# Eight-core transformer layer: small inputs in one transfer, earlier weight halves, layer norms by pieces, the D term from channel-major x

## The chip, the cores and the metric

The kernel runs on all 8 cores of one Trainium2 chip. Each core works on its own share of the batch, and the shares do not communicate. The metric is the device time of the slowest core, in microseconds (us), from its first to its last instruction. Each core has five engines: TensorE (PE in the profile, its weight loads PEld), VectorE (DVE), ScalarE (ACT), GpSimd (POOL) and SyncE (SP, which here only issues transfers).

Some executions fall into a slow state, in which one die shows a lower granted clock and the time is some per cent longer.

## The reference, cut to what matters

One layer with two groups of tokens that share all weights. Per core there are 1024 latent tokens and 512 context tokens (two sequences of 256). In the kernel, group `GB` is the latent one (row tiles 0 to 7, chunks 0 and 1 of x) and `GA` the context one (row tiles 8 to 11, chunk 2).

```python
h    = x * (1 + sc1) + sh1                    # shift, scale, gate: silu(cond) @ w_ada + b_ada
q, k, v, g, z, xbc, dt = split(h @ w_in)
o_ret = silu(g) * rms_norm(bidir_scan(q, k, v))            # 4 retention heads, chunkwise scan
xs, B, C = split(silu(depthwise_conv(xbc)))
y     = bidir_scan(C, B, xs * dt) + d_skip * xs            # 8 SSD heads; d_skip * xs is the "D term"
o_ssd = rms_norm(y * silu(z)) * ssd_norm_w
x     = layer_norm(ALPHA * x + g1 * (concat(o_ret, o_ssd) @ w_out), ln1_g, ln1_b)      # LN1
h2    = x * (1 + sc2) + sh2
x     = layer_norm(ALPHA * x + g2 * ((silu(h2 @ w_gate) * (h2 @ w_up)) @ w_down), ln2_g, ln2_b)   # LN2
```

## The kernel before

The kernel is a Python program that first collects operations with their reads and writes, then orders them by a list scheduler of its own, and lays all tiles into one arena of SBUF. The tables `LV` (priorities, lower first), `RING` (how many buffers a tile rotates through) and `LD` (which event starts a load) tune the result. I call order plus addresses *the plan*. It is fixed when the kernel is built, so it can be read by building the kernel, without a chip. Where I say "the built kernel" below, that is what was read.

Two tiles whose lifetimes do not overlap in the plan may share addresses, and the later one then waits for every operation on the earlier one:

```python
old, new = (b, c) if t1 <= u0 else (c, b)        # two tiles that share addresses
for f in firsts[new]:
    extra.setdefault(f.idx, set()).update(old.ops)
```

The start, cut: transfers on SyncE's queue in program order, and those that GpSimd issues when their `after` is done.

```python
P.dma(SP, cols, ...); P.dma(SP, cst, ...)         # [cut] constants from DRAM
ada_f32(2)                                        # w_ada slab 2, two halves
xT_load(2, 0); half_load("w_in0", w0, w_in_d[0], 0)
P.dma(SP, smalls, ...); P.dma(SP, w_dtf, ...)     # small inputs
xT_load(0, 0); ada_f32(3); xT_load(2, 1)
o_w0 = half_load("w_in0", w0, w_in_d[0], 1); xT_load(0, 1)
w_in[1] = slab_load("w_in1", ..., after=[o_w0])
ada[0] = slab_load("ada0", ..., after=[xTo[(0, 1)]])
ada[1] = slab_load("ada1", ..., after=[w_in[1][1]])
xT_load(1, 0, after=[ada[0][1]]); xT_load(1, 1, after=[ada[0][1]])   # the last x chunk
```

The residual and the normalisation, the same code for LN1 (groups of four tiles) and LN2:

```python
def residual(dst, banks, xres, gate, s, i):
    for half in range(2):
        hs = slice(half * 512, half * 512 + 512)
        tt(dst[:, hs], banks[half], gate[:, hs], ALU.mult)
        stt(dst[:, hs], xres[:, hs], ALPHA, dst[:, hs], ALU.mult, ALU.add, accum_out=s[:, half, i:i + 1])
    act(rjn(), dst, AF.Square, accum_out=s[:, 2, i:i + 1])         # rjn(): output that nobody reads
def normalise(dsts, s):                                            # one chain of small steps for four tiles
    # [cut] six small VectorE steps on 128x4
    tt(c[7], c[6], mhalf[:, 0:1].to_broadcast([128, n]), ALU.pow, POOL)
    stt(c[8], c[3], -1.0, c[7], ALU.mult, ALU.mult)
    # [cut] affine(dst) by halves
```

After the context tiles' LN1 come 32 transposes, and then the feed-forward's first matmuls for the context. These are the *filler*: plenty of TensorE work that needs nothing from the latent group, to be run while the latent group's retention waits on other engines.

## Time and profile before

Median 744.0 us (743.6 to 745.7). The view of cores:

```profile
core 3: 744.4 us, clock 0.964
core 7: 729.0 us, clock 0.979
```

The windows view of core 3, the slowest. Columns: the stretch and its length, then busy us (and instruction count) of PE, PEld, DVE, ACT, POOL, then the granted TensorE clock, DMA share and GB/s.

```profile
0.00:40.00 40.00, 13.21 (x108) 6.35 (x109) 22.16 (x93) 19.21 (x32) 2.67 (x12) 0.90 0.90 275
40.00:60.00 20.00, 20.00 (x166) 9.97 (x165) 8.34 (x25) 10.47 (x22) 1.58 (x3) 0.94 1.01 157
60.00:80.00 20.00, 6.38 (x113) 3.94 (x111) 5.73 (x18) 6.19 (x10) 2.54 (x11) 0.74 0.95 207
80.00:150.00 70.00, 69.14 (x504) 39.20 (x505) 45.32 (x109) 56.18 (x92) 30.17 (x65) 0.98 0.56 108
150.00:300.00 150.00, 135.07 (x1175) 78.77 (x1172) 120.18 (x198) 82.33 (x129) 84.20 (x97) 0.94 0.54 104
300.00:340.00 40.00, 35.21 (x289) 21.61 (x288) 36.99 (x69) 26.83 (x39) 23.95 (x22) 1.00 0.80 177
340.00:400.00 60.00, 57.82 (x330) 31.56 (x329) 44.62 (x98) 32.83 (x50) 15.26 (x17) 1.00 0.27 72
```

Read it as a list of where TensorE stands idle: 26.8 us in the first 40, 13.6 between 60 and 80 (the *hole*, with DMA at 0.95), 14.9 between 150 and 300, 4.8 between 300 and 340. From 408 us on it is dense.

The chain of waits says why the hole is there. Columns: start, length, what was waited for or done.

```profile
10.56 28.18 DMA arena<-xT
39.34 15.80 DMA arena<-w_ada
55.79 22.66 DMA arena<-xT
80.12 37.16 PE psum L634 x258
```

The last x chunk is under way until 78.5 us, and TensorE starts dense work on it at 80.

The end, from the timeline (start, length, engine, line, operation, output<-input, count, and in brackets the idle time before it and what ended it):

```profile
725.78 3.62 PE L634 MATMUL psum<-arena 128*128 128x512 bf16 x16
736.93 0.55 POOL L684 TENSOR_TENSOR arena<-arena 128x1 f32<-128x1 f32 x1 [0.43 <-DVE arena L684]
737.95 0.81 ACT L659 ACTIVATE arena<-arena 128x512 f32<-128x512 f32 x1 [3.75 <-DVE arena L698]
738.90 3.36 POOL L684 TENSOR_TENSOR arena<-arena 128x512 f32<-128x512 f32 x2 [1.43 <-ACT arena L659]
```

The last matmul ends at 729.4 us and the span at 744.4: a bare tail of 15.0 us.

### The profile page before, as it was taken

What the parts mean: (1) busy time and instruction counts of PE and PEld (TensorE: products, weight loads), DVE (VectorE), ACT (ScalarE), POOL (GpSimd) and SP (SyncE); (2) the same over time, 40 slices, a digit from 0 to 9 for tenths busy, and PEclk for the clock granted to TensorE, in tenths of its full rate; (3) what the DMA queues carried; (4) which work ended last, traced back from release to release, by engine and by line L of the source; (5) the groups of instructions that cost most, each with busy time, mean ns of one, the idle gap of its engine ahead of it and who ended that gap; (6) DMA issues with size and microseconds to landing.
All of it is one profiled execution on the core that took longest, in us unless ns stands there. A gap on an engine that the chain in (4) does not pass through costs nothing.

```text
span 744.4 us, 13000 instructions; the slowest of 8 cores (729.0 to 744.4 us)
## 1 busy us (share of the span) xinstructions
PE 666.2 (89%) x4212; PEld 342.3 (46%) x4212; DVE 404.5 (54%) x817; ACT 302.2 (41%) x478; POOL 291.4 (39%) x312
## 2 busy tenths in 40 slices
PE   0595699999978988989999999999999999999991
PEld 0243455545643456546445444444444444444440
DVE  6533249879876887898587212121121211366865
ACT  2654698686673333587447211111111110132121
POOL 0001315696364355566101299800000000059876
PEclk9888799999998998999999999999999999999996
DMA  8999726681697063980035133545300046002212
GB/s 241 333 145 220 147 37 113 143 169 26 120 156 131 2 126 75 251 173 30 29 113 114 57 58 57 113 82 106 82 1 1 1 106 163 1 28 85 86 58 85
DMA packets 15043, 75.68 MB, mean 102 GB/s; under 512 B 2960, under 2 KB 3216, under 8 KB 8320
## 3 DMA queue, kind: packets, MB, share of 16 engines
q0 software_dynamic: 5440, 40.77, 31.1%
q1 hardware_dynamic: 9536, 34.07, 14.0%
q8 instruction: 36, 0.59, 0.3%
q14 instruction: 31, 0.25, 0.1%
HBM read 107.03 MB, written 8.40 MB: 155 GB/s over the span
## 4 chain that ended last, share of the span: by engine, by line
PE 64%; DMA 12%; issue 8%; DVE 7%; POOL 4%; ACT 1%; SPq 1%; DVEq 0%; POOLq 0%; ACTq 0%
PE psum L634 64%; DMA arena<-xT 7%; DVE arena L684 4%; POOL arena L684 4%; DMA arena<-w_ada 4%; DVE arena L698 1%; SPq L191 1%; ACT arena L659 1%; DMA arena<-arena 1%; PE psum L637 1%; DVE arena L719 1%; DVE arena L722 1%; DVE arena L709 0%; DVEq L518 0%; POOL arena L191 0%
## 5 line engine op out<-in xcount | busy, mean ns | idle before, releaser
L634 PE MATMUL psum<-arena 128*128 128x512 bf16 (+6 forms) x4104 | 655.2, 318 | 63.0 <-ACT arena L659 29.5
L634 PEld LDWEIGHTS psum<-arena 128*128 128x128 bf16 (+1 forms) x4104 | 330.8, 99 | 384.0 <-issue 100.5
L684 POOL TENSOR_TENSOR arena<-arena 128x512 f32<-128x512 f32 (+6 forms) x204 | 257.4, 1282 | 185.1 <-DVE arena L684 116.3
L659 ACT ACTIVATE arena<-psum 128x512 bf16<-128x512 f32 (+2 forms) x180 | 99.8, 571 | 222.5 <-PE psum L634 204.3
L684 DVE TENSOR_TENSOR arena<-arena,psum 128x512 bf16<-128x512 bf16 (+3 forms) x134 | 86.6, 653 | 181.0 <-PE psum L634 175.8
L659 ACT ACTIVATE arena<-arena 128x512 bf16<-128x512 f32 (+8 forms) x156 | 107.5, 717 | 174.4 <-DVE arena L698 117.8
L684 DVE TENSOR_TENSOR arena<-psum,arena 128x512 bf16<-128x512 f32 (+5 forms) x202 | 127.8, 650 | 57.4 <-PE psum L634 48.1
L659 ACT ACT_TABLE_LOAD x48 | 61.6, 1283 | 26.2 <-PE psum L634 20.7
L698 DVE SCALAR_TENSOR_TENSOR arena<-arena 128x512 f32<-128x512 f32 (+2 forms) x60 | 43.9, 732 | 15.2 <-POOL arena L684 11.6
L684 DVE TENSOR_TENSOR arena<-arena 128x1 f32<-128x1 f32 (+10 forms) x87 | 38.6, 444 | 10.2 <-PE psum L634 3.2
L191 POOL DMA_DIRECT2D arena<-w_down x4 | 2.2, 538 | 101.5 <-PE psum L634 101.5
L659 ACT ACTIVATE arena<-psum,arena 128x512 bf16<-128x512 f32 (+2 forms) x58 | 35.9, 650 | 13.4 <-PE psum L634 8.8
L191 POOL DMA_DIRECT2D arena<-w_in x10 | 5.9, 590 | 57.5 <-DMA arena<-w_in 34.4
L709 DVE CAST arena<-psum 128x512 bf16<-128x512 f32 (+2 forms) x29 | 17.7, 622 | 17.7 <-PE psum L634 15.4
L709 DVE CAST arena<-arena 128x512 bf16<-128x512 f32 (+8 forms) x39 | 21.5, 557 | 10.7 <-DMA arena<-w_ada 4.3
L191 POOL DMA_DIRECT2D arena<-w_gu x11 | 6.4, 578 | 39.3 <-issue 20.7
L709 POOL CAST arena<-arena 128x2 bf16<-128x2 f32 x48 | 8.5, 220 | 33.8 <-DVE arena L709 16.4
L719 DVE SCALAR_TENSOR_TENSOR arena<-arena 128x512 f32<-128x512 f32 x25 | 19.6, 828 | 0.7
L690 DVE TENSOR_SCALAR arena<-arena 128x128 bf16<-128x128 f32 (+6 forms) x79 | 16.6, 260 | 5.0 <-ACT arena L659 4.1
L722 DVE TENSOR_SCALAR arena<-arena 128x512 bf16<-128x512 f32 x27 | 12.8, 510 | 11.6 <-DMA arena<-xT 11.5
L1279 DVE COPY_PREDICATED psum<-arena,psum 128x512 f32<-128x512 uint16 x24 | 16.6, 691 | 3.0 <-PE psum L634 2.7
L637 PE MATMUL psum<-arena 128*128 128x128 f32 (+1 forms) x108 | 14.4, 275 | 0.2 <-DVE arena L684 0.2
(20 smaller groups left out, 58.1 us busy)
## 6 DMA issues: line engine op xcount, KB each, us to landing
arena<-w_gu POOLq DMA_DIRECT2D x11, 1024.0 KB, 10.5
arena<-w_in POOLq DMA_DIRECT2D x10, 1024.0 KB, 11.8
arena<-w_ada POOLq DMA_DIRECT2D x10, 1024.0 KB, 15.2
arena<-xT SPq DMA_DIRECT2D x6, 1024.0 KB, 20.0
arena<-x SPq DMA_DIRECT2D x12, 512.0 KB, 4.9
arena<-w_down POOLq DMA_DIRECT2D x4, 1408.0 KB, 15.9
y<-arena SPq DMA_DIRECT2D x11, 512.0 KB, 2.7
arena<-w_ada SPq DMA_DIRECT2D x4, 1024.0 KB, 15.3
```

The source lines that it names most:

```text
L191: o = self.add({eng: (0.9 if eng == POOL else 0.45, lambda e: e.dma_start(out=R(out), in_=R(in_)))}, [in_], [out], after=after)
L634: return P.add({PE: (c, lambda e: e.matmul(R(out), lhsT=R(lhsT), rhs=R(rhs), start=start, stop=stop))}, [lhsT, rhs], [out])
L637: return P.add({PE: (0.12, lambda e: e.transpose(out=R(out), in_=R(in_), identity=R(ident_f)))}, [in_, ident_f], [out])
L659: fn = lambda e: e.activation(out=R(out), in_=R(in_), func=func, **{k: R(v) for k, v in kw.items()})
L684: fn = lambda e: e.tensor_tensor(out=R(out), in0=R(in0), in1=R(in1), op=op)
L690: fn = lambda e: e.tensor_scalar(out=R(out), in0=R(in0), scalar1=R(s1), scalar2=None, op0=op0)
L698: fn = lambda e: e.scalar_tensor_tensor(out=R(out), in0=R(in0), scalar=R(scalar), in1=R(in1), op0=op0, op1=op1, **{k: R(v) for k, v in kw. ...
L709: alts[g] = (vcost(g, out, [in_], "copy"), lambda e: e.tensor_copy(out=R(out), in_=R(in_)))
L719: lambda e: e.scalar_tensor_tensor(out=R(out), in0=R(in_), scalar=R(scale), in1=R(bias).to_broadcast([128, n_]), op0=ALU.mult, op1=ALU.add))
L722: lambda e: e.tensor_scalar(out=R(out), in0=R(in_), scalar1=R(scale), scalar2=R(bias), op0=ALU.mult, op1=ALU.add))
L1279: P.add({DVE: (0.7, lambda e, eb=eb, ef=ef, mk_=mk_: e.copy_predicated(R(eb), R(mk_), R(ef)))}, [mk_, ef, eb], [eb])
```

## The change

Intent: take small transfers and constants out of the queue at the start; load all weights that the first two chunks need before the last x chunk, so that the hole is filled; make the last tile's LN2 short; halve the matmuls of the D term. The new tiles did not fit beside the old plan, so rings, priorities and triggers were tuned again. The core of the diff, with cuts marked:

```diff
@@ start
-    P.dma(SP, cst, cf_d[:, 0:392])
+    iota(diff, 1, 0, -1, 0.5); ...; ts(ident_f, diff, 0.0, ALU.is_equal)      # [cut] constants made on chip
+    half_load("ada2", b, w_ada_d[2], 0)
+    P.dma(SP, cols, cols_d[:, :])                                  # all small inputs in one
+    ada[2] = (b, half_load("ada2", b, w_ada_d[2], 1))
-    w_in[1] = slab_load("w_in1", w_in_d[1], 4096, after=[o_w0])
-    ada[0] = slab_load("ada0", w_ada_d[0], 4096, after=[xTo[(0, 1)]])
-    ada[1] = slab_load("ada1", w_ada_d[1], 4096, after=[w_in[1][1]])
-    xT_load(1, 0, after=[ada[0][1]])
+    w_in[1] = slab_load("w_in1", w_in_d[1], 4096, after=[xTo[(2, 1)]])
+    ada[0] = slab_load("ada0", w_ada_d[0], 4096, after=[xTo[(2, 1)]])
+    ada[1] = slab_load("ada1", w_ada_d[1], 4096, after=[xTo[(2, 1)]])
+    for q in range(2):                                             # chunk 1, behind them on POOL's queue
+        xTo[(1, q)] = P.dma(POOL, xT[(1, q)], ..., after=[xTo[(2, 1)]])
@@ first projections: both slabs of chunks 2 and 0 before chunk 1
+    for ck in (2, 0): EV["p0" + "BxA"[ck]] = proj(0, ck)
+    for ck in (2, 0): EV["p1" + "BxA"[ck]] = proj(1, ck)
+    proj(0, 1); EV["p1C"] = proj(1, 1)
@@ D term
-        mm(y[:, h * 64:h * 64 + 64], dI3[:, h, :], xs_tm[t][:, h * 64:h * 64 + 64], False, True)    # 8 per tile
+        mm(y[:, c * 128:c * 128 + 128], xsT[(g, c)][:, tok], dI[:, c * 128:c * 128 + 128], True, False)   # 4 per tile
@@ LN1: by tile
+            s, junk = rst(), rjn()
+            for half in range(2):
+                piece(x1[t], banks[half], xr, gate, H[half], s, half, junk)    # square of half a row
+            moments(s, 2)                                                      # small steps on 128x1
+            tt(col(s, S_RSTD), col(s, S_MSQ), mhalf[:, 0:1], ALU.pow, POOL)
+            # [cut] affine by halves
@@ LN2: last tile in pieces of 512, 256, 256 columns
+            act(col(s, S_LN), col(s, S_NVAR), AF.Ln, scale=-1.0)
+            act(col(s, S_RSTD), col(s, S_LN), AF.Exp, scale=-0.5)
+            stt(w[:, hs], u[t][:, hs], col(s, S_MEAN), ln2[:, hs], ALU.subtract, ALU.mult)
+            stt(u[t][:, hs], w[:, hs], col(s, S_RSTD), ln2[...], ALU.mult, ALU.add)
@@ tables (cut)
-RING = dict(... yb=1, xw=3, Sd=3, ... hB=3, ... kt=2, ... xr=3)
+RING = dict(... yb=3, xw=2, Sd=2, ... hB=2, ... kt=3, ... xr=2)
-LD = dict(... xr1="b1", xr0="oA", ...)      # x rows for the context residual: latent head 1's projections done
+LD = dict(... xr1="b2", xr0="b3", ...)      # now: latent head 2's
-OPT = dict(rope="")
+OPT = dict(rope="q")
```

## The prediction

> **What bounds it now.** The view of cores: 729.0 to 744.4 us; core 3 is slowest. Its page has TensorE busy 666 of 744 us, so 78 us idle. Windows and timeline of core 3 place them:
> - Start: dense work proper begins at 36.9 us; TensorE is busy 13.2 of the first 40 us, DMA share near 1: transfer-bound.
> - Hole, 60 to 80 us: busy 6.4 of 20, DMA share 0.95. TensorE waits for a scaled x chunk; the last xT transfer, queued beside the second w_ada slab, lands at 78.5 us. Core 7, the quickest, is busy 12.9 there.
> - 150 to 400 us: about 22 us idle in pieces, VectorE 80 to 90% busy.
> - 408 to 729 us: dense, 0.2155 us per 512-column matmul. Nothing to win.
> - Tail: the last matmul ends at 729.4, the span at 744.4: 15 us. Residual pieces, a 1.06 us square, small VectorE steps, a POOL power, a 0.8 us affine, two multiply/add pairs (1.7 us per POOL step), the store.
>
> **The change, costed.**
> 1. Start: 196 KB of constants, the row and w_dt transfers leave the queue; cols goes behind the first w_ada half. At the 322 GB/s of 10 to 20 us, everything comes about 1 us earlier. The 786 KB selector load goes too, but nothing waited for it after 79 us.
> 2. Hole: both shift slabs of w_ada and w_in's second slab come before the last x chunk; the second slab's projection of chunk 0 (32 x 0.2155 = 6.9 us) and the context convolutions (80 x about 0.11 = 8.6 us) can run before it. The dense run from 37 should reach about 78 us, when chunk 1 lands. Gain about 12 us on the slowest core, 7 on a quick one, including a cold start: the Trainium skill, "TensorE: Matmul & The Clock Gate", Part 1, says that an idle array falls to half clock and needs about 3.4 us to warm; the trace agrees (matmuls 0.43 us apart after 22 and 37 us). Against it: POOL-issued loads start beside the last SP-issued halves and may cost 1 to 2 us at 37.
> 3. D term: 96 64-column matmuls become 48 128-column ones: about 1 us of TensorE.
> 4. LN1 by tile; new priorities, rings, load triggers; rope's q halves on ScalarE and POOL: 0 to 5 us, could be negative. I take 2.
> 5. Tail: 256-column residual 0.9, square 0.65, small steps 0.5, Ln and Exp 0.6 (no table load between them at 22 us), VectorE pieces 3, store 2: about 8 us against 15. Gain 6 to 7, fully exposed. POOL's multiplies leave, so VectorE's 1.1 to 1.8 us steps should take 0.7: the Trainium skill, "SBUF — State Buffer", "Who interferes with whom", says VectorE with two SBUF inputs contends with a POOL operation that reads SBUF.
>
> Sum: 1 + 12 + 1 + 2 + 6.5, about 22. 744 - 22 = **722 us**, 8 in 10 within 709 to 735. Faster by over 2% (below 729): 0.75; within 2%: 0.22; slower: 0.03.
>
> **Right or wrong in the profile.** Windows 60 to 80: TensorE over 17 of 20 busy on the slowest core, cores closer together. First dense run still from 36 to 38 us. Tail 7 to 9 us from last matmul to end. TensorE busy about 663 us. Last stretch: no 512-wide POOL operations. Idle of 150 to 400: 15 to 24 us.
>
> **What would make it wrong.** The filled hole is given back in the mixed stage because VectorE, not TensorE, bounds it there; new waits on weights whose triggers moved; w_in's second half slowed by sharing; denser TensorE work lowering the granted clock; a table load in the tail.

## More of the kernel before

The experiments' texts call the latent group "batch".

One more stretch, for comparison with after: TensorE between the end of the head projections and the context's transposes (the group with f32 128x128 tiles).

```profile
336.09 2.83 PE L634 MATMUL psum<-arena 128*128 128x128 bf16 x46 [2.00 <-DVE arena L684]
338.76 0.61 PE L637 MATMUL psum<-arena 128*128 128x128 f32 x4
```

TensorE waits 2.0 us here, the longest wait in the 20 us before the transposes, which start at 338.8 us.

## The result, and the profile after

After: 734.5 us median (734.1 to 738.0). The ratio to before is 0.988 (0.985 to 0.991). Ratios here are the mean time of one kernel's fast runs over that of the other's fast runs of the same rounds, so not quite the ratio of the medians quoted. The gain is 9.5 us, where 22 were forecast: the time is inside the range, at its upper edge, but "within 2%".

```profile
core 1: 733.4 us, clock 0.969
```

The windows of core 1, the slowest of after, with the same columns as before:

```profile
0.00:40.00 40.00, 14.66 (x109) 6.74 (x110) 25.87 (x88) 16.74 (x30) 10.61 (x23) 0.91 0.93 282
40.00:60.00 20.00, 20.00 (x172) 10.33 (x171) 11.73 (x32) 12.16 (x21) 1.52 (x3) 1.00 1.00 209
60.00:80.00 20.00, 16.68 (x189) 11.32 (x188) 8.72 (x27) 14.16 (x24) 8.30 (x45) 0.83 1.02 197
80.00:150.00 70.00, 69.71 (x508) 38.91 (x506) 47.20 (x112) 63.75 (x100) 31.28 (x38) 1.00 0.40 84
150.00:300.00 150.00, 136.46 (x1197) 82.73 (x1197) 119.58 (x203) 83.82 (x131) 92.61 (x104) 0.99 0.73 128
300.00:340.00 40.00, 21.97 (x167) 13.38 (x165) 30.68 (x71) 18.87 (x37) 18.96 (x18) 0.74 0.27 89
340.00:400.00 60.00, 59.15 (x309) 32.11 (x309) 47.04 (x126) 35.84 (x65) 12.64 (x15) 0.97 0.33 89
```

Subtract the PE column of before from it, stretch by stretch. To 150 us TensorE has done 12.3 us more: the hole is filled (16.7 of 20, where 6.4 were). Between 150 and 300 it gains 1.4. **Between 300 and 340 it loses 13.2.** To 400 it regains 1.3. The TensorE work in all is 1.6 us less (the D term; 666.2 and 664.6 on the two pages), and the tail is 7.6 us shorter. The sum, 12.3 + 1.4 - 13.2 + 1.3 + 1.6 + 7.6 = 11.0, is the difference of the two spans (744.4 - 733.4). The loss at 300 to 340 us is not that of one core: TensorE is busy 34.4 to 35.3 of these 40 us on the eight cores of before, and 20.7 to 22.0 on the eight of after.

The start and the hole in the chain of waits of after:

```profile
7.20 28.11 DMA arena<-w_in
...
36.59 27.07 PE psum L632 x252
```

Dense work starts at 36.6 us, 0.3 before that of before (36.9), and no wait for the last x chunk is left in this stretch.

The tail of after, from the timeline:

```profile
721.76 4.20 PE L632 MATMUL psum<-arena 128*128 128x256 bf16 x37
728.25 2.99 DVE L696 SCALAR_TENSOR_TENSOR arena<-arena 128x512 f32<-128x512 f32 x6
728.43 0.50 ACT L657 ACTIVATE arena<-arena 128x1 f32<-128x1 f32 x2 [0.79 <-DVE arena L690]
```

The last matmul ends at 725.96; 7.4 us follow. Ln and Exp take 0.50 us together, with no table load between them. The Trainium skill, "ScalarE: Activation LUTs", section "Table sets: the hidden batching unit", says that one set holds both; the trace agrees.

And the new hole, from the timeline of 300 to 350 us. DVE L696 are the residuals, ACT 128x512 bf16<-128x512 f32 with arena on both sides the context tiles' squares:

```profile
306.23 1.75 DVE L696 SCALAR_TENSOR_TENSOR arena<-arena 128x512 f32<-128x512 f32 x1
...
312.69 0.68 DVE L696 SCALAR_TENSOR_TENSOR arena<-arena 128x512 f32<-128x512 f32 x1
...
327.76 0.63 ACT L657 ACTIVATE arena<-arena 128x512 bf16<-128x512 f32 x1 [1.33 <-issue]
...
336.99 0.58 ACT L657 ACTIVATE arena<-psum 128x512 bf16<-128x512 f32 x1
...
337.81 2.29 PE L632 MATMUL psum<-arena 128*128 128x512 bf16 x13 [11.09 <-DVE arena L690]
...
340.70 5.64 PE L635 MATMUL psum<-arena 128*128 128x128 f32 x32 [0.59 <-DVE arena L717]
```

TensorE idles 11.1 us before 337.8. The profile puts the wait down to VectorE, but the operation that ended just before is the ScalarE read of PSUM at 336.99 (retention's own). It stood in ScalarE's queue behind squares and affines of the context's LN1. The built kernel confirms both: the first of these 13 matmuls reads what that ScalarE operation writes, and ScalarE's order has the eight squares and three affines of the context's LN1 before it. The first square starts at 327.8 us although its residual was ready at 308.0 (306.23 + 1.75). The context's transposes start at 340.7, 1.9 us *later* than before (338.8), although TensorE came 12 us earlier to this point. So the filler is not there when the head projections run out.

### The profile page after: what moved, and what is told of

Same layout as the page of the kernel before. It is cut to its first block, busy times and chain, and to the rows that moved or that the text cites. A ratio compares the mean times of both kernels' runs of the same rounds, so it can differ in the third digit from the quotient of the medians.

```text
span 733.4 us, 13130 instructions; the slowest of 8 cores (722.6 to 733.4 us)
## 1 busy us (share of the span) xinstructions
PE 664.6 (91%) x4186; PEld 346.7 (47%) x4186; DVE 411.7 (56%) x896; ACT 309.1 (42%) x546; POOL 236.9 (32%) x277
## 3 DMA queue, kind: packets, MB, share of 16 engines
q1 hardware_dynamic: 8960, 31.77, 12.9%
## 4 chain that ended last, share of the span: by engine, by line
PE 78%; DMA 10%; issue 4%; DVE 4%; ACT 2%; POOL 2%; SPq 1%; DVEq 0%; ACTq 0%; POOLq 0%
PE psum L632 76%; DMA arena<-w_in 5%; DMA arena<-w_ada 4%; DVE arena L682 2%; PE psum L635 2%; DVE arena L696 1%; POOL arena L682 1%; ACT arena L657 1%; ACT L657 1%; SPq L192 1%; DVE arena L690 0%; POOL arena L192 0%; POOL arena L707 0%; DVE arena L717 0%; DVE arena L720 0%
## 5 line engine op out<-in xcount | busy, mean ns | idle before, releaser
L632 PE MATMUL psum<-arena 128*128 128x512 bf16 (+5 forms) x4078 | 652.7, 319 | 60.5 <-ACT arena L657 22.5
L632 PEld LDWEIGHTS psum<-arena 128*128 128x128 bf16 x4078 | 333.6, 99 | 374.8 <-issue 86.9
L682 POOL TENSOR_TENSOR arena<-arena 128x512 f32<-128x512 f32 (+5 forms) x160 | 197.1, 1249 | 138.9 <-ACT arena L657 39.2
L657 ACT ACTIVATE arena<-arena 128x512 bf16<-128x512 f32 (+7 forms) x200 | 113.5, 588 | 145.4 <-DVE arena L696 92.7
L682 DVE TENSOR_TENSOR arena<-psum,arena 128x512 f32<-128x512 f32 (+6 forms) x187 | 116.6, 643 | 42.7 <-PE psum L632 37.1
L696 DVE SCALAR_TENSOR_TENSOR arena<-arena 128x512 f32<-128x512 f32 (+1 forms) x99 | 71.0, 752 | 4.3 <-DVE arena L682 2.3
L690 DVE TENSOR_SCALAR arena<-arena 128x1 f32<-128x1 f32 (+2 forms) x112 | 23.1, 216 | 31.1 <-ACT arena L657 21.6
L707 DVE CAST arena<-psum 128x512 bf16<-128x512 f32 (+2 forms) x42 | 25.2, 605 | 14.3 <-PE psum L632 10.7
L682 DVE TENSOR_TENSOR arena<-arena 128x8 f32<-128x8 f32 (+8 forms) x55 | 22.3, 412 | 4.6 <-PE psum L632 3.2
L707 DVE CAST arena<-arena 128x256 bf16<-128x256 f32 (+8 forms) x35 | 17.4, 500 | 8.6 <-DMA arena<-w_ada 5.1
L688 DVE TENSOR_SCALAR arena<-arena 128x128 bf16<-128x128 f32 (+5 forms) x78 | 17.1, 266 | 6.0 <-ACT arena L657 5.4
```

The source lines that it names most:

```text
L632: return P.add({PE: (c, lambda e: e.matmul(R(out), lhsT=R(lhsT), rhs=R(rhs), start=start, stop=stop))}, [lhsT, rhs], [out])
L657: fn = lambda e: e.activation(out=R(out), in_=R(in_), func=func, **{k: R(v) for k, v in kw.items()})
L682: fn = lambda e: e.tensor_tensor(out=R(out), in0=R(in0), in1=R(in1), op=op)
L688: fn = lambda e: e.tensor_scalar(out=R(out), in0=R(in0), scalar1=R(s1), scalar2=None, op0=op0)
L690: fn = lambda e: e.tensor_scalar(out=R(out), in0=R(in0), scalar1=R(s1), scalar2=R(s2), op0=op0, op1=op1)
L696: fn = lambda e: e.scalar_tensor_tensor(out=R(out), in0=R(in0), scalar=R(scalar), in1=R(in1), op0=op0, op1=op1, **{k: R(v) for k, v in kw. ...
```

## The experiments

Three theories at the outset. **A**: the loss at 300 to 340 us is made by the plan (false memory waits, late triggers, order of ScalarE's work) around the context tiles' LN1. **B**: the mixed stage is bounded by VectorE and the elementwise work, so any lead of TensorE is lost there. **C**: LN1 by tile is too slow in itself.

| run | ratio to before | median of fast runs, us | context transposes start, us |
|---|---|---|---|
| after | 0.988 | 734.5 | 340.7 |
| e5 after again | 0.988 | 736.3 | 342.8 |
| e1 LN2 only | 0.989 | 739.7 | 340.0 |
| e2, e9 own address | 0.981, 0.983 | 735.0, 733.1 | 335.8, 333.2 |
| e3 own address, early x rows | 0.978 | 732.2 | 332.5 |
| e4 context LN1 left out | 0.972 | 727.9 | 332.3 |
| e10 LN1 by four | 0.973 | 725.9 | 330.6 |
| e11 priorities only | 0.980 | 731.0 | 334.7 |
| e12 context by four | 0.979 | 728.4 | 333.8 |
| e13 latent by four | 0.975 | 725.5 | 327.7 |
| e14 by four and priorities | 0.969 | 721.1 | 326.1 |
| e6 pad in after | 1.003 | 746.9 | 353.5 |

The runs went to several chips, on which before took 744 to 750 us in its fast runs, so compare ratios, not medians. Those of e5 and e6 are worked out from one fast run of before. The last column is that of the profiled run's slowest core. It is good to about 3 us: e2 and e9, the same kernel, differ by 2.6, and e10 and e12, whose built plans are alike up to the latent group's output stage, by 3.2.

**e1_tail.** The kernel before with LN2 alone in the new form.

```diff
-            residual(u, banks, x1[t], gate, st_, t % grp); ...; normalise(us, st_)
+            piece(u[t], ps, x1[t], gate, ..., half + p, jk[t]); moments(s, 1 + parts); ...   # as in the change
```

> The kernel before with only the second layer norm (its residual, moments and output) in the new form; everything else of before, its plan to 408 us included, is kept. All theories agree here, since nothing after 408 us waits for VectorE but the tail: last matmul to end of span 15.0 -> 7.4 us (7 to 8.5), TensorE busy between 300 and 340 us still about 35 of 40, total 736.5 us (735.5 to 738), that is -7.5 against before. If the total moves by less than 6, the 7.6 us read from the tail of after are not all the tail's.

Measured 0.989 (0.986 to 0.991), 739.7 us where before took 748.4 on that chip. The last matmul ended at 730.7 and the span at 738.4: 7.7 us. This one part gives as much as the whole change, so all the rest of the change together gave nothing. Theories do not differ here; the size of the tail term is confirmed.

**e2_own, e9_own_again.** In after, the squares' unused output shares its addresses with two retention states of the latent group; that is read off the kernel's own address table, not off a trace. So the squares wait for the last matmuls that read these states. Here it is moved to free memory, and every other address stays. The order does not, although the expectations of e2 and e3 say so: the scheduler runs once more after the move, and in the built kernels 679 of TensorE's 4182 places differ from after, from 301 us of the plan on, and ScalarE and VectorE are ordered anew from there too (in e3 from about 252 us on).

```diff
-    act(junk[:, hs], dst[:, hs], AF.Square, accum_out=...)
+    o = act(jv, dst[:, hs], AF.Square, accum_out=...); P.own.append((o, jv))      # context tiles only
+    nb = Buf(self, "ljunkA", old.n, old.dt); nb.off = 208448                      # after placement
```

> The kernel after, its order of instructions and all other addresses held; only the unused output of the eight squares of the context tiles' LN1 goes to an address of its own, so that these squares no longer wait until the matmuls that read head 2's retention states are done. Theory A (the give-back at 300 to 340 us is an accident of order and memory around the context tiles' LN1): the squares start when their residuals are there (at about 308 to 320 us instead of 327.8), retention's square is no longer behind them, TensorE busy in 300 to 340 us rises from 22 to 26 or more, total 729 to 732.5. Theory B (VectorE and the elementwise chain bound the stretch 100 to 340 whatever the order): total within 1.5 us of after, 733 to 736. Theory C (the LN1 by tile with its many small steps is itself what is too long): a part only, TensorE 22 to 25, total 732 to 735.

> e2_own once more, on another chip and beside other kernels, since after itself did not run on the chip of e2_own: theory A ratio to before 0.979 to 0.985 and TensorE busy 26 or more of 40 between 300 and 340 us; no effect of the false wait would be 0.986 to 0.990 and 20 to 24.

Measured 0.981 (0.978 to 0.985) and 0.983 (0.981 to 0.985), against 0.988 of after: about 0.5%, 4 us. The timeline of e9:

```profile
309.23 0.63 ACT L689 ACTIVATE arena<-arena 128x512 bf16<-128x512 f32 x1 [1.22 <-DVE arena L728]
...
311.54 0.58 ACT L689 ACTIVATE arena<-psum 128x512 bf16<-128x512 f32 x1
312.64 0.63 ACT L689 ACTIVATE arena<-arena 128x512 bf16<-128x512 f32 x1 [0.53 <-DVE arena L728]
...
333.19 2.72 PE L667 MATMUL psum<-arena 128*128 128x128 f32 x12
```

The first square starts at 309.2 instead of 327.8 us, the transposes at 333.2 instead of 340.7. TensorE is busy 27.4 to 27.7 us between 300 and 340, where after has 22. Here a read of PSUM (311.54) stands between two squares, where in after all eight came before the read that mattered. So taking the shared address away, with the order that the scheduler then makes, is worth about 4 us, less than the 7.5 by which the transposes move in e9 (4.9 in e2), and it is not all of the loss. How much is the wait itself and how much the new order, these runs can't tell.

**e3_own_earlyx.** As e2, and the context's x rows asked for earlier. Here too the order is made anew.

```diff
+    o.deps.discard(EV["b2"]); o.deps.add(EV["a3"])      # the four "xr1" loads, after placement
```

> As e2_own, and the four x row tiles of the context residual are asked for earlier (when the context head's third projection is done, not the batch head's third), the order of instructions on the compute engines held. Theory A: the residuals move from 306-320 us to before 305, the context tiles' transposes from 340.7 to 335 or earlier, the feed-forward's filler matmuls from 346 to 340 or earlier, TensorE busy in 300 to 340 us 27 or more, total 724 to 731. Theory B: nothing gained, 733 to 736, with VectorE 18 or more of 20 busy in 280 to 320. Theory C: 731 to 734.

Measured 0.978 (0.976 to 0.981), about 3 us better than e2 and e9. (The intervals of e2 and e3 overlap, but on their common chip every fast run of e3, up to 732.4, was below every one of e2, from 733.0.) The step that A named came true only in part: the residuals of the first two tiles start at 263.1 and 294.0 us (in after the first starts at 306.2), but the last two come at 311.4 and 321.4. The rows pass through a ring of two, and the load of the last ones is issued at 314.3, just after the third tile's residual has ended (314.2). The timeline:

```profile
263.06 0.68 DVE L734 SCALAR_TENSOR_TENSOR arena<-arena 128x512 f32<-128x512 f32 x1
...
293.97 1.67 DVE L734 SCALAR_TENSOR_TENSOR arena<-arena 128x512 f32<-128x512 f32 x1
...
321.40 1.69 DVE L734 SCALAR_TENSOR_TENSOR arena<-arena 128x512 f32<-128x512 f32 x1
```

The transposes start at 332.5 and long filler matmuls at 339.0, as A had it, and TensorE is busy 29.0 us in the window. The time on a chip where before takes 744 would be 727.8, inside A's range. VectorE is busy 18.3 of 20 us in 300 to 320 but 17.1 in 320 to 340; the gain was there to be had all the same.

**e4_no_ln1c.** Its output is wrong, which doesn't matter for the time.

```diff
+    order = {e: [o for o in order[e] if o not in dead] for e in ENGS}     # dead: 44 operations of the context's LN1
```

> Wrong result on purpose: the kernel after, order held, with the 44 operations of the context tiles' LN1 after the residual (8 squares, 24 small VectorE steps, 4 powers, 8 affines) left out, so that the transposes take the residual itself. An upper bound of what that chain holds up. Theory A and C: the hole of 11 us at 327 to 338 goes, TensorE busy in 300 to 340 us 30 or more, total 722 to 727. Theory B: the chain's VectorE time is only about 5 us, so 730 to 735.

Measured 0.972 (0.969 to 0.976): 11.5 us better than after through the two ratios. TensorE is busy 30.3 us in the window. This bounds what that chain holds up, and it is about the size of the loss (13.2). It cannot tell A from C. Here the order was held (the built kernel has that of after, without the 44). The record's check let this run pass as correct all the same, so a passed check says little about this part of the result.

**e5_after_again** and **e6_pad_after, e7_pad_before, e8_pad_own_earlyx.** Is TensorE's lead worth anything? 56 unneeded matmuls, into the PSUM bank that is about to be filled, take it away again.

```diff
+        for _ in range(56): self.alone[o.idx](e)        # start=True, stop=True, just ahead of chunk 1's first projection
         return fn(e)
```

> The kernel after, unchanged, as a control on the chip of this batch (its other chip ran before 0.6% slower than the first): ratio to before 0.985 to 0.991, hole at 300 to 340 us again with TensorE busy 20 to 24 of 40.

> The kernel after with 56 unneeded 512-column matmuls (12.1 us of TensorE) just ahead of the first projection of x chunk 1, at about 71 us: the head start that the filled hole gave is taken away, nothing else is changed. Theory A (the 300 to 340 us hole is made by the order and triggers of this plan, which all count TensorE's steps): the whole mixed stage shifts with TensorE, the hole stays nearly as wide, total +8 to +12 against after (742 to 747 on a chip where after takes 734.5). Theory B (VectorE and the elementwise chain bound the stretch, TensorE's lead is lost anyway): the hole shrinks by most of the 12 us, total +0 to +4.

> The same 56 matmuls in the kernel before, at the same place (its chunk 1 lands at 78 us). Is TensorE's lead worth anything under the old plan? Theory A: yes, before's mixed stage follows TensorE with few idle us, so +8 to +12 (752 to 756 where before takes 744), TensorE busy in the 40 us after 312 us again about 35. Theory B: VectorE catches up, +0 to +5.

> The same 56 matmuls in e3_own_earlyx, whose hole is smaller: theory A +9 to +12 against e3_own_earlyx (ratio to before about 0.991 to 0.995 instead of 0.978). Theory B +0 to +5 (ratio 0.978 to 0.985).

Only one of seven runs of before was fast (744.5). After again: 733.7 to 736.8 in four fast runs. Padded after: 746.3 to 747.7 in four fast runs, so 11.2 us slower by the means. The timeline of the padded kernel:

```profile
72.37 12.03 PE L646 MATMUL psum<-arena 128*128 128x512 bf16 x54
...
350.59 2.29 PE L645 MATMUL psum<-arena 128*128 128x512 bf16 x13 [11.26 <-DVE arena L705]
353.48 5.16 PE L650 MATMUL psum<-arena 128*128 128x128 f32 x32 [0.60 <-DVE arena L732]
```

The pad is 12.03 us, and the idle time before the 13 matmuls is 11.26 us as in after (11.09), 12.8 us later (10.7 later than in e5, the control). The hole did not shrink: it moved with TensorE. That goes against B, which had +0 to +4. It does not refute B alone, since the pad holds VectorE's work back as well. The first 150 us of e6 and of e5:

```profile
0.00:150.00 150.00, 119.97 (x932) 66.08 (x949) 83.12 (x245) 96.66 (x158) 42.55 (x97) 0.95 0.68 160
0.00:150.00 150.00, 119.44 (x957) 67.03 (x973) 94.03 (x259) 106.89 (x174) 52.05 (x109) 0.95 0.71 169
```

VectorE has done 83.1 us of work where the control has done 94.0, so a VectorE that bounds the stretch from there on would end later too. What speaks clearly against B is e11 below: the same operations, in another plan, end sooner. e6 also says that the head start reached the end nearly whole (11 of 12 us): without it, the change would be no faster than before (1.003, with one fast run of before). The padded before ran 759.0 in its only fast run (+14.5), the padded e3 744.6 and 745.6. Both are above what either theory had (+14.5 where A had 8 to 12; ratio 1.001 where A had 0.991 to 0.995), with one fast run to compare with. They go against B, with the same reserve as e6, and their excess I leave unexplained.

**e10_ln1_by_four.** After with the old form of LN1; the plan is made anew.

```diff
-            s, junk = rst(), rjn(); ...; piece(...); moments(s, 2); ...
+            residual(x1[t], banks, xr, gate, st_, t % grp)
+            if (t + 1) % grp == 0: normalise([...], st_)
```

> The kernel after with LN1 again in the form of before: one whole-row square and one chain of small steps for four tiles; the plan is made anew with after's priorities and triggers. Theory C (the LN1 by tile is what holds the stretch up): the hole closes to before's size (TensorE 32 or more of 40 in 300 to 340 us), ratio to before 0.975 or lower. Theory A (triggers, priorities and memory of the new plan): the hole stays, TensorE 20 to 28 of 40, ratio 0.982 to 0.992.

Measured 0.973 (0.971 to 0.976): as C had it in time. TensorE is busy 28.2 us in the window, which is at the upper edge of A's figure and not C's 32. The window proved a poor measure, since kernels that run ahead before 300 us have less left to do in it. The start of the transposes is the better one, 330.6 us:

```profile
320.69 1.06 ACT L658 ACTIVATE arena<-arena 128x1024 bf16<-128x1024 f32 x1 [1.68 <-DVE arena L697]
321.65 0.19 ACT L658 ACTIVATION_READ_ACCUMULATOR arena<-arena 128x1 f32 x1
...
330.55 1.30 PE L636 MATMUL psum<-arena 128*128 128x128 f32 x5 [1.15 <-ACT arena L658]
```

The last residual ends at 320.4 us in after and at 320.5 here. Here the last square starts at once, at 320.7, and the transposes follow 9.9 us later. In after all eight half-row squares were still to be done then; they began at 327.8, and the transposes came 12.9 us after that. But the plan is another one too: the built kernel still has the squares' output over two of the latent group's retention states, but orders the work on these states earlier.

**e11_reprio.** The same operations as after, five priorities and one trigger.

```diff
-LV = dict(... retB=1.1, evA=0.9, outA=1.6, outB=1.5, evoA=0.7 ...); LD = dict(... xr0="b3" ...)
+LV = dict(... retB=1.3, evA=1.7, outA=1.3, outB=0.05, evoA=0.5 ...); LD = dict(... xr0="z11" ...)
```

> The kernel after with the same operations and only five priorities and one trigger of its plan changed (batch retention behind, context evacuations and the context LN1 earlier, batch x rows earlier). Theory A: the hole is a matter of the plan, so TensorE gets to 27 or more of 40 in 300 to 340 us, ratio to before 0.974 to 0.982. If the operations themselves make the hole: 0.985 to 0.990.

Measured 0.980 (0.978 to 0.982), TensorE busy 27.4 us in the window. The transposes:

```profile
334.69 5.35 PE L631 MATMUL psum<-arena 128*128 128x128 f32 x24 [1.13 <-ACT arena L653]
```

About 6 us of the loss go by the plan alone, with the same operations, as A had it. That is not order alone: the addresses come out anew too, and in the built kernel the squares' output no longer lies over retention states, so part of these 6 us can be the 4 of e2 and e9.

**e12_ctx_by_four, e13_batch_by_four.** The two groups apart.

```diff
+    def out_stage(g, pool, lv): return (out_four if g == GA else out_tile)(g, pool, lv)      # e12; e13: g == GB
```

> LN1 by four for the four context tiles, by tile for the eight batch tiles; the plan up to the batch's out stage is that of e10_ln1_by_four. Theory C (form of the context LN1): as e10, ratio to before 0.971 to 0.976, TensorE 27 or more of 40 in 300 to 340 us. If the batch tiles' form made e10's gain: 0.981 to 0.988.

> The reverse: the context tiles by tile, the batch tiles by four; the plan that comes out places the context squares' unused output over nothing that is still live and gives the squares no run of eight in a row. Theory A (false wait and order): TensorE 27 or more of 40 in 300 to 340 us, ratio 0.971 to 0.979. Theory C (context LN1 by tile is slow in itself): 0.982 to 0.989, TensorE 20 to 25.

Measured: e12 0.979 (0.976 to 0.982), 6 us better than after, between the two expectations; e13 0.975 (0.972 to 0.978), as A had it, though TensorE's 25.9 us in the window fell short of 27, for the reason given at e10: it had done 140.2 us of work between 150 and 300 already, where after did 136.5. The timeline of e13:

```profile
304.22 0.63 ACT L658 ACTIVATE arena<-arena 128x512 bf16<-128x512 f32 x1
...
327.72 1.51 PE L636 MATMUL psum<-arena 128*128 128x128 f32 x6 [0.39 <-issue]
```

The context's LN1 is by tile here, as in after, and yet its transposes start at 327.7 us, earlier than in e10 and e12, where it is by four. So C falls as the sole cause: by tile is not too slow in itself when its squares run as their residuals come.

**e14_four_reprio.** The version all this points to: e10's LN1 with e11's priorities and trigger.

```diff
 # e10, and:
+LV and LD as e11; RING sq=3
```

> e10_ln1_by_four with the five priorities and the trigger of e11_reprio and one ring deeper by one: the version that beats both if A and C add up. Ratio 0.960 to 0.972 (716 to 725 us), TensorE 31 or more of 40 in 300 to 340 us. If both act on the same wait they do not add and it is 0.971 to 0.976.

Measured 0.969 (0.966 to 0.972), 720.1 and 722.0 us in the two fast runs, where before took 744.0 to 745.6 on that chip. It passes the record's check, and these two runs are below every run of both kernels; the other four were in the slow state, so its verdict on record is "unclear".

```profile
326.12 5.67 PE L632 MATMUL psum<-arena 128*128 128x128 f32 x28 [3.44 <-DVE arena L679]
```

Transposes at 326.1 us, the earliest of all. TensorE's 27.9 us in the window missed the expected 31, as above; by 400 us it had done 348.3 us of work, where after had done 338.6. The two gains add for the most part: 1.5% for LN1 by four and 0.8% for the priorities, 1.9% together.

## Why the prediction was wrong, point by point

- **Start, +1.** Hardly shown: dense work began 0.3 us earlier (36.9 to 36.6).
- **Hole, +12.** Right. With the start, 12.3 us by 150 us where 13 were forecast. In detail it fell a little short: TensorE was busy 16.7 of 20 us where "over 17" was forecast, and the dense run from 36.6 ended at 63.7 us (36.59 + 27.07) and not at about 78. The pad shows that these us are worth 11 at the end. I had read the chain correctly: the last x chunk was the wait, and there was work to put before it.
- **D term, +1.** Not shown by itself. TensorE's total fell by 1.6 us, but by shape (the view of lines, `--by-form`) the 64-column matmuls went from 192 and 7.8 us to 96 and 7.0, and the 128-column ones from 656 and 53.8 us to 704 and 62.1. The busy times also carry the granted clock, so the gain of the D term alone can't be read from them.
- **LN1 by tile and the new priorities, rings and triggers, "I take 2". This is the step that failed.** The stretch from 150 to 400 us (32.4 us idle, where I had 15 to 24) gave 1.4 - 13.2 + 1.3 = -10.5 us, so the term was off by 12.5. I had allowed that it "could be negative", with a size of 0 to 5 us. I treated a retuned plan as noise of a few us, when it decided whether the filler was ready.
- **Tail, +6.5.** Right: 7.6 in the profiles, and 1.1% by e1 alone.

Without the failed term the profiles give 12.3 + 1.6 + 7.6 = 21.5, about what was forecast. The failed one took 10.5 back.

What would make it wrong was named as well: "the filled hole is given back in the mixed stage because VectorE, not TensorE, bounds it there". The first half came true, the reason did not. VectorE was *less* busy in 300 to 340 us than before (30.7 against 37.0 us), and the same operations ended about 6 us sooner in another plan (e11). What the runs show in its place:

1. The squares of the context's LN1 waited on an address they shared with tiles that were still in use. Giving that output an address of its own, with the order that the scheduler then makes, gains about 4 us (e2, e9).
2. Asking earlier for their x rows, whose trigger the new plan had moved one head later, gains about 3 us more (e3), though with the ring of two it helps the first two tiles alone.
3. ScalarE had eight squares and three affines ahead of a read that TensorE waited for. What a new plan around this is worth: 6 us with the same operations (e11), 11 with LN1 by four (e10), 6 with only the context tiles by four (e12), 10 with only the latent tiles by four (e13). These runs change order and addresses together.

These gains overlap, since each brings the context's transposes forward. In the table, leaving out e1 and e6, which lack the head start, the time falls roughly as the transposes come earlier, from 340.7 us and 0.988 to 326.1 us and 0.969; within 2 or 3 us of one another the order does not always hold. What stays open is how the loss divides between the shared address and the order, since no run changes one alone, and how much of e10's gain is the form of LN1 and how much the plan that came with it: each change of form changes the plan, and I have no pair of kernels that differ in the form alone. Also open is the reverse test, the new start with the old plan, since the two do not fit into memory together (built with the old tables, the new kernel asks for 219,744 of 212,800 bytes).

The granted clock fell with the hole: 0.74 in 300 to 340 us, where before had 1.00. The Trainium skill, "TensorE: Matmul & The Clock Gate", Part 1, says that an idle array is throttled after about 3.4 us; the trace agrees: after the gap of 11.1 us the clock is 0.50 (337.8 to 341 us). It was already 0.62 at 315 to 320, where TensorE was busy 0.97 of 5 us. So it is a consequence of the idle time, not its cause.

## What to carry to other kernels

When a change moves one engine ahead by some us, find the work that it will run into and ask when *that* will be ready: a lead is kept only if everything that fills the next stretch comes earlier too. An unused output is not free: it needs an address, and if that address is shared, its writer waits for tiles that it has nothing to do with. And when a kernel has to be tuned again to make room, give the retuning a term of its own, with the size that the schedule shows and not a small number. Here it could have been read before any run: in the built plan of after, the scheduler's own times have TensorE idle for 11.5 us (314.8 to 326.3) ahead of these same 13 matmuls, whereas after the first 32 us of before's plan no wait is longer than 2.1 us.

## What the Trainium skill lacked or had wrong

- "SBUF — State Buffer", section "Who interferes with whom", says that VectorE with two SBUF inputs contends with a GpSimd operation that reads SBUF. The trace agrees and gives a size that the section lacks for this pair: the same 128x512 f32 residual took 0.68 us alone (at 312.69 in after) and 1.75 us (at 306.23) while GpSimd ran 128x512 f32 operations on SBUF (304.56 to 309.11).
- "ScalarE: Activation LUTs" gives no cost for reading out an accumulated sum. Here its record lasts 0.19 us, but half-row squares in a row (327.76, 328.38, 329.00 us in after) start every 0.62 us with the reads between them, so two cost 1.24 us a tile, where one of a whole row costs 1.15 with its read (320.69 to 321.84 in e10).
- No page warns that the profile's name for a wait can miss a ScalarE operation queued behind others: the 11.09 us before 337.81 in after are put down to VectorE, but the ScalarE operation at 336.99 writes what the first matmul reads (the built kernel's dependencies).
